# Two changes of issue order in a decoder layer: factor splits of the first matrix pair, and the place of one background job

## The chip, the cores and the metric

The kernel runs on one core of a Trainium2 chip. The metric is device time in microseconds of one execution; three executions of the kernel before gave 1956.08, 1957.77 and 1959.51, so its median is 1957.77 us. The engines are named as in the profile: PE multiplies matrices, DVE and ACT work on vectors, POOL does little here, SP issues the DMA transfers.

## The reference

One layer of a decoder over 512 tokens of width 2048, in fp32:

```python
for l in range(DEPTH):                       # DEPTH = 1
    h = rms_norm(x, norm1_g[l])
    proj = h @ w_in[l]
    qa, ka, va, ra, ga, qb, kb, vb = jnp.split(proj, split_points, axis=-1)
    gate_pre = (ga @ gla_gate_w2[l] + gla_gate_b[l]).astype(jnp.float32)
    log_g = jax.nn.log_sigmoid(gate_pre) / GLA_GATE_TAU
    out_a = gla_mixer(...)                   # gated linear attention, 4 heads
    ...
    out_b = dilated_mixer(...)               # dilated window attention, 8 heads
    mix = jnp.concatenate([out_a, out_b], axis=-1)
    x = x + mix @ w_out[l]
    h2 = rms_norm(x, norm2_g[l])
    x = x + (jax.nn.silu(h2 @ w_gate[l]) * (h2 @ w_up[l])) @ w_down[l]
```

The hidden width of the last line is 5632. Nearly all the work is in the five matrix products.

## The kernel before

**Products.** Each fp32 product is done in a rounded format with a correction: every operand is split in a *high* part, cast by ACT, and a *low* part, the remainder, computed by DVE. For the left factor that is `Operand.split` (L175 the cast, L176 the remainder); for a weight tile the two lines are L311 and L315, or L403 and L407 in the first pair, with results `wh` and `wl`. The matrix products are grouped in pairs of 512-column blocks and carried out by a seven-product scheme in the manner of Strassen: products P1 to P7, whose left factors are the quarters A11, A12, A22 of the operand or their sums and differences S1 to S4, and whose right factors are weight quarters or differences of them (L397 in the first pair, L227 later). Each product runs over four groups of the inner dimension, numbered 0 to 3. One group of one product is an *item*: eight matmuls with `wh` (two terms, the left factor's high and low part) and then four with `wl`.

**First pair.** `first_pair` handles the first pair by hand. Its products come in the order P1, P2, P5, P6, P3, P7, P4, so 28 items numbered k from 0: k = 8 is P5 group 0, k = 9 is P5 group 1 (it needs S1 of group 1, called S1.1), and P4, which needs A22, is k = 24 to 27. In each item the weight splits for the item after are issued, then the eight high matmuls, then one row of the table `FIRST` (the row of item k is number k + 2, counted from 0), then the four low ones. A row is a list of tokens: `S1.1` splits a factor, `+S1.1` computes the sum that is split (L730), `A22.1` splits that quarter, `t.` tokens transpose input, `sq.` tokens are squares for the norm (L643 on ACT), `gate.0` and `gate.1` are `ranks`, 32 small matmuls each (L775), of which gate.1 multiplies the factors A22 and S1. Every engine works strictly in the order in which its instructions were written.

**Later pairs.** They run through `stream`, which calls the pair's `step` between the high and low matmuls of an item. A step advances generators on the list `background`; the first on the list that does not answer "wait" is served first. An item whose factor is not yet split forces the background on until it is.

**The end of the out-projection.** The last item of the second out-projection pair is P4 group 3; after it comes the gate/up pair that I call ffn0 (P1 groups 0 to 3, then P5, P6, P3 and so on). While the out-projection is being closed, rows of x1 are finished on DVE (L1414, L1411), squared (L1447) and scaled (L1422) on ACT, transposed on PE (L1135), copied by ACT with the norm's gain (L1146) and stored to a DRAM tile `xn_d` (L1150). They come back as operand tiles: `early_jobs` loads a tile `top` in two halves of the tokens (L1196), splits its first half as A11, subtracts (L1234) and splits the difference as S3. `late_jobs` loads other tiles (L1250, L1196 into `r`) and makes S1, S2 and S4 and A22. For groups 2 and 3 both jobs are appended to `background` when `which == 1 and half == 1` in `final_out`. Groups 0 and 1 were listed before, as `operand_jobs`.

**Transfers.** SP issues all of these loads and stores in one line, the weight loads (L184) among them, and before each it waits until the transfer eight before it has landed.

Of the kernel before, what the change touches and what calls it, by code (L numbers as in the profile page):

```python
# [43 lines left out]
    "t.l4 +S3.0 t.u1",  # L44
    "t.u3 t.u4 A12.0 A11.3 A12.1 A11.2",
    "t.l5 S2.0 t.l3 +S1.2 +S4.0",
    "S1.2 t.u7 A22.1 t.u5 A12.2",
    "A12.3 t.l6 +S2.2",
    "+S3.2 sq.1.2 S4.0",
    "t.l7 t.l2 +S1.3",  # L50
    "S1.3 sq.1.3",
    "+S1.1 sq.0.1 sq.0.3 A22.2 sq.1.0 +S2.3 sq.0.2",
    "S1.1 sq.2.3 sq.1.1 sq.0.0 g2",
    "normA.0 sq.3.1 sq.3.2 sq.2.1 +S2.1 sq.3.0",
    "A22.3 +S3.1 normB.0 S2.1 normC.0 +S3.3 gprep",
    "S2.2 sq.2.0 seeda sq.3.3 sq.2.2",
    "S2.3 normA.1 +S4.3 normB.1 +S4.1 gate.0",
    "normC.1 +S4.2",
    "closea S3.2 seedb gate.1",
    "S4.1 S3.1",  # L60
    "",
    "S4.2 S4.3",
    "S3.0",
    "seedc",
    "",
    "S3.3",
    "closec",
    "",
    "",
    "",  # L70
# [38 lines left out]
def block_kernel(ctx: ExitStack, tc: tile.TileContext, ins, out):  # L109
# [19 lines left out]
    def nm(s):  # L129
        uid[0] += 1  # L130
        return f"{s}_{uid[0]}"
# [7 lines left out]
    def work(tag, shape=(P, 512), bufs=1):  # L139
        return mp.tile(list(shape), F32, name=nm(tag), tag=tag, bufs=bufs)  # L140

    def const(shape, name):
        return cp.tile(list(shape), F32, name=name, tag=name)
# [345 lines left out]
    background = []  # L489
# [4 lines left out]
    def later(units, fn, hold=False):  # L494

        deferred.append([units, fn, hold])
# [78 lines left out]
    g2 = const([P, 16], "g2")  # L575
# [119 lines left out]
    for g in range(4):  # L695
        for b in (2 * g, 2 * g + 1):
            if g < 3:
                t = apool.tile([P, 2, 512], F32, name=nm("xT"), tag="A")
# [495 lines left out]
    def part_load(t, src, half):  # L1194
        assert (id(src), half) in done
        load(t, src[:, :, half * 256 : (half + 1) * 256])  # L1196
        return t

    def staged(items, ahead=1, cost=1.0, groups=3):

        queue = []
        for keys, fetch, use in items:
            while len(queue) > ahead or not all(key in done for key in keys):
                if queue and ripe(queue[0][2], groups):
                    t, u, when = queue.pop(0)
                    u(t)
                    yield cost
                else:
                    yield WAIT
            queue.append((fetch(), use, now[0]))  # L1210
        while queue:
            if ripe(queue[0][2], groups):
                t, u, when = queue.pop(0)
                u(t)
                yield cost
            else:
                yield WAIT

    def early_jobs(op, groups, tops, flip):

        h0, h1 = (1, 0) if flip else (0, 1)
        items = []
        for g in groups:
            hold = []

            def fetch(g=g, hold=hold):
                t = apool.tile([P, 2, 2, 256], F32, name=nm("top"), tag="A")
                part_load(t[:, 0], tops[g], h0)
                part_load(t[:, 1], tops[g], h1)
                hold.append(t)  # L1230
                return t

            def differ(t, g=g):
                nc.vector.tensor_tensor(t[:, 1], t[:, 0], t[:, 1], op=ALU.subtract)  # L1234
                op.split("S3", g, t[:, 1])

            items.append((
                [(id(tops[g]), 0), (id(tops[g]), 1)], fetch, lambda t, g=g: op.split("A11", g, t[:, 0])
            ))
            items.append(([], lambda hold=hold: hold[0], differ))  # L1240
        return staged(items, 2, 0.5)
# [150 lines left out]
    def residual_loads(rows, c0, src, room="qk"):  # L1392

        res = []
        for m in range(2):
            if room == "L":
                r = work("L", bufs=2)
            elif room == "C":
                r = cpool.tile([P, 512], F32, name=nm("rows"), tag="C")
            else:  # L1400
                r = work(room[m])
            load(r, src(rows[m], c0))
            res.append(r)
        return res

    def residual(tiles, acc_, rest):
        res = []
        for m in range(2):
            r = rest[m]
            if tiles is None:  # L1410
                nc.vector.tensor_tensor(halves(r), unfolded(acc_[m]), halves(r), op=ALU.add)  # L1411
                res.append(r)
            else:
                nc.vector.tensor_tensor(tiles[m], tiles[m], r, op=ALU.add)  # L1414
                res.append(tiles[m])
        return res
# [9 lines left out]
    def final_out(second):  # L1426
        rest_of = {}

        def ahead(half, which):
            tok = 1 - half  # L1430
            rest_of[half, which] = residual_loads(
                [2 * tok, 2 * tok + 1], 512 * (2 * second + which),
                lambda t, c: x[t * P : (t + 1) * P, c : c + 512],
                "C" if (half, which) == (1, 0) else "qk",
            )

        def final(half, which, tiles, acc_):
            tok = 1 - half
            rows = [2 * tok, 2 * tok + 1]
            ch = 2 * second + which  # L1440
            last = tiles is None
            tiles = residual(tiles, acc_, rest_of.pop((half, which)))
            for m in range(2):
                t = rows[m]
                store(x1_d[t][:, 512 * ch : 512 * ch + 512], tiles[m])
                jk = work("st", (P, DV), bufs=2).bitcast(mybir.dt.bfloat16)
                nc.scalar.activation(  # L1447
                    jk, tiles[m], AF.Square, accum_out=ss2[:, t, ch : ch + 1]
                )
            if second:  # L1450
                def scaled():
                    turn = scaled_store(tiles, rows, tok, xn_d[2 * ch : 2 * ch + 2], 4 * ch)
                    later(2, turn)

                if last:
                    later(4, scaled)
                else:
                    scaled()
                if which == 1 and half == 1:
                    background.append(early_jobs(opn, (2, 3), tops, False))  # L1460
                    background.append(late_jobs(opn, ((2, 3),), tops, bots, False))
                if which == 0 and half == 1:
                    output_scales()
            elif which == 0 and half == 1:
                nc.vector.tensor_tensor(part2, ss2[:, :, 0], ss2[:, :, 1], op=ALU.add)
                first_scale()
                background.append(first_columns())
                background.append(operand_jobs(opn, (0, 1), tops, bots))

        final.ahead = ahead  # L1470
        return final
# [51 lines left out]
    opn = Operand(4)  # L1523
    tops = [xn_d[2], xn_d[3], xn_d[6], xn_d[7]]
# [200 lines left out]
```

## Time and profile before

| what | value |
|---|---|
| median of three executions | 1957.77 us |
| the profiled execution | 1956.06 us |
| its span | 1953.9 us, so 2.2 us lie outside it |
| mean granted clock of PE | 0.999 |
| PE busy | 1922.4 us (98%) |
| DVE busy | 1651.5 us (85%) |
| ACT busy | 1095.6 us (56%) |

Start times are in microseconds from the span's start. In a row of the timeline the first two columns are start and duration of a group, then engine, line, operation, and "out<-in" with the tile names; `x8` counts instructions; `[2.19 <-DVE AS L176]` says that the engine stood idle 2.19 us before the group and what ended that. In a table of windows the columns after the length are the busy times of PE, PE's weight load, DVE, ACT and POOL with instruction counts, then PE's granted clock, the busy share of the DMA engines and GB/s.

### The profile page before, as it was taken

The page shows a single profiled execution, that of the slowest core. Times are in us where ns is not written, and L with a number is a line of the kernel's source. Part 1 is how long each engine was busy: PE and PEld are TensorE (multiplying, and loading weights), DVE is VectorE, ACT ScalarE, POOL GpSimd, SP SyncE. Part 2 cuts the span into 40 slices and gives each one's busy share as a digit, 9 for nine tenths or more (in the row PEclk, how much of TensorE's full clock was granted, in tenths as well). Part 3 has the DMA queues.
Part 4 walks back from the last instruction along what each step waited for, and adds up shares of the span by engine and source line. Part 5 has one row for each costly group of instructions (what it writes and reads, how often), then busy time and mean ns, then how long its engine had stood idle before and what let it go on. Part 6 is the DMA issues. An engine that isn't in the chain of part 4 may idle for free.

```text
span 1953.9 us, 25802 instructions
## 1 busy us (share of the span) xinstructions
PE 1922.4 (98%) x9226; PEld 1670.1 (85%) x9226; DVE 1651.5 (85%) x1855; ACT 1095.6 (56%) x1602; POOL 59.1 (3%) x79
## 2 busy tenths in 40 slices
PE   8999999999999999999999999999999999999999
PEld 6888888888888878888888888888888888888888
DVE  8997787867899889878878878878879989989987
ACT  8564564666775776544545545445446646546443
POOL 0000240010000000000000000000000000000000
PEclk9999999999999999999999999999999999999999
DMA  8458355475676695564564553553555865955762
GB/s 280 135 163 276 104 182 157 130 211 181 194 242 195 207 310 168 165 183 126 176 173 127 175 167 124 176 165 129 173 161 163 300 199 185 317 172 180 258 211 69
DMA packets 237801, 362.02 MB, mean 185 GB/s; under 512 B 18294, under 2 KB 96575, under 8 KB 237672
## 3 DMA queue, kind: packets, MB, share of 16 engines
q1 hardware_dynamic: 237320, 360.16, 58.0%
q8 instruction: 72, 1.18, 0.3%
q14 instruction: 57, 0.47, 0.1%
q10 hardware_dynamic: 352, 0.21, 0.0%
HBM read 298.16 MB, written 64.51 MB: 186 GB/s over the span
## 4 chain that ended last, share of the span: by engine, by line
PE 87%; DVE 7%; DMA 2%; issue 2%; ACT 1%; SPq 0%; POOL 0%; DVEq 0%; ACTq 0%
PE acc L355 78%; PE acc L423 3%; DVE wl L315 2%; DVE wa L227 1%; PE bank L1135 1%; PE bank L990 1%; PE bank L1022 1%; DVE AS L176 1%; DMA x<-in_x 1%; ACT wh L311 0%; PE bank L775 0%; PE bank L1015 0%; DMA top<-xn_d 0%; PE bank L925 0%; PE bank L908 0%
## 5 line engine op out<-in xcount | busy, mean ns | idle before, releaser
L355 PE MATMUL acc<-wh,AS 128*128 128x512 f32 x3008 | 711.4, 379 | 0.0
L355 PEld LDWEIGHTS acc<-wh,AS 128*128 128x128 f32 x3008 | 569.2, 189 | 80.2 <-ACT wh L311 0.5
L311 ACT CAST wh<-wa 128x1024 fp32r<-128x1024 f32 x376 | 394.1, 1049 | 401.6 <-PE acc L355 372.1
L355 PE MATMUL acc<-wh,AA 128*128 128x512 f32 x2256 | 534.4, 380 | 2.2 <-ACT wh L311 1.9
L315 DVE TENSOR_TENSOR wl<-wa,wh 128x1024 fp32r<-128x1024 f32 x376 | 459.2, 1225 | 73.0 <-ACT wh L311 41.2
L355 PEld LDWEIGHTS acc<-wh,AA 128*128 128x128 f32 x2256 | 426.8, 189 | 63.9 <-ACT wh L311 3.3
L355 PE MATMUL acc<-wl,AS 128*128 128x512 f32 x1504 | 395.7, 386 | 6.9 <-DVE wl L315 6.7
L355 PEld LDWEIGHTS acc<-wl,AS 128*128 128x128 f32 x1504 | 279.5, 189 | 57.7 <-DVE wl L315 16.9
L355 PE MATMUL acc<-wl,AA 128*128 128x512 f32 x1128 | 295.9, 385 | 1.2 <-DVE wl L315 1.0
L355 PEld LDWEIGHTS acc<-wl,AA 128*128 128x128 f32 x1128 | 210.0, 189 | 32.2 <-DVE wl L315 3.7
L311 ACT CAST wh<-wb 128x1024 fp32r<-128x1024 f32 x94 | 98.6, 1049 | 125.7 <-PE acc L355 120.3
L311 ACT CAST wh<-wc 128x1024 fp32r<-128x1024 f32 x94 | 98.4, 1047 | 112.9 <-PE acc L355 105.6
L311 ACT CAST wh<-wd 128x1024 fp32r<-128x1024 f32 x94 | 98.6, 1049 | 106.6 <-PE acc L355 104.6
L227 DVE TENSOR_TENSOR wa<-wc,wa 128x1024 f32<-128x1024 f32 x94 | 115.1, 1227 | 49.8 <-DMA wc<-in_w_gate 27.7
L315 DVE TENSOR_TENSOR wl<-wd,wh 128x1024 fp32r<-128x1024 f32 x94 | 114.8, 1224 | 39.0 <-ACT wh L311 33.3
L315 DVE TENSOR_TENSOR wl<-wc,wh 128x1024 fp32r<-128x1024 f32 x94 | 115.2, 1225 | 34.0 <-ACT wh L311 33.8
L315 DVE TENSOR_TENSOR wl<-wb,wh 128x1024 fp32r<-128x1024 f32 x94 | 114.2, 1223 | 5.5 <-ACT wh L311 5.5
L227 DVE TENSOR_TENSOR wb<-wd,wb 128x1024 f32<-128x1024 f32 x94 | 115.3, 1227 | 0.7 <-DMA wd<-in_w_in 0.3
L227 DVE TENSOR_TENSOR wa<-wb,wa 128x1024 f32<-128x1024 f32 x94 | 114.0, 1223 | 0.8
L227 DVE TENSOR_TENSOR wa<-wd,wa 128x1024 f32<-128x1024 f32 x94 | 113.6, 1226 | 0.0
L272 DVE SCALAR_TENSOR_TENSOR seed<-acc,rs,seed 128x512 f32<-128x512 f32 x96 | 70.8, 749 | 23.3 <-PE acc L355 23.3
L256 ACT ACTIVATE seed<-acc,rs 128x512 f32<-128x512 f32 x96 | 60.6, 682 | 0.8 <-PE acc L355 0.8
(316 smaller groups left out, 1369.6 us busy)
## 6 DMA issues: line engine op xcount, KB each, us to landing
wa<-in_w_gate SPq DMA_DIRECT2D x44, 512.0 KB, 4.5
wb<-in_w_up SPq DMA_DIRECT2D x44, 512.0 KB, 4.5
wd<-in_w_up SPq DMA_DIRECT2D x44, 512.0 KB, 4.4
wc<-in_w_gate SPq DMA_DIRECT2D x44, 512.0 KB, 3.6
wc<-in_w_in SPq DMA_DIRECT2D x32, 512.0 KB, 3.8
wa<-in_w_in SPq DMA_DIRECT2D x24, 512.0 KB, 5.3
wb<-in_w_in SPq DMA_DIRECT2D x24, 512.0 KB, 5.8
wd<-in_w_in SPq DMA_DIRECT2D x24, 512.0 KB, 6.5
```

The lines of the kernel that those rows point to most:

```text
L176: nc.vector.tensor_tensor(a[:, :, 1, :], src, a[:, :, 0, :].bitcast(F32), op=ALU.subtract)
L227: nc.vector.tensor_tensor(src, self.quarter(one, g), src, op=ALU.subtract)
L256: nc.scalar.activation(halves(t), unfolded(src[m]), AF.Copy, scale=self.scale(half, m))
L272: nc.vector.scalar_tensor_tensor(halves(seed[m]), unfolded(src[m]), self.scale(half, m), halves(seed[m]), op0=ALU.mult, op1=ALU.add,)
L311: nc.scalar.copy(high[k], sources[k])
L315: nc.vector.tensor_tensor(low[k], sources.pop(k), high[k].bitcast(F32), op=ALU.subtract)
L355: nc.tensor.matmul(p.dst[prod][m], a[:, jj, hl, m * P : (m + 1) * P], folded(w[:, jj, :]), start=fresh and g == 0 and len(terms) == 2 and ...
L423: recent["pe"] = nc.tensor.matmul(dst[prod][m], a[:, jj, hl, m * P : (m + 1) * P], folded(w[:, jj, :]), start=fresh and g == 0 and len(ter ...
L990: nc.tensor.matmul(lp[:, :n], qh[:, b * P : (b + 1) * P], kh[:, :n], start=True, stop=True)
L1022: nc.tensor.matmul(op, vh[:, k, :], lgs[b][:, k * P : (k + 1) * P], start=(k == 0), stop=(k == b))
L1135: nc.tensor.transpose(bk[:, jj, m * P : (m + 1) * P], tiles[m][:, f : f + P], ident)
```

## The change

In `FIRST`, A22.1, A22.2 and A22.3 are split ten or more rows later, S1.1 is split right behind its sum and so ahead of four squares, and gate.1 moves from row 16 to row 25, that is from item k = 14 to k = 23. In `final_out`, `early_jobs` of groups 2 and 3 is put at the head of the background list, not at its end.

```diff
@@ -44,27 +44,27 @@
     "t.l5 S2.0 t.l3 +S1.2 +S4.0",
-    "S1.2 t.u7 A22.1 t.u5 A12.2",
+    "S1.2 t.u7 t.u5 A12.2",
     "A12.3 t.l6 +S2.2",
     "+S3.2 sq.1.2 S4.0",
     "t.l7 t.l2 +S1.3",
     "S1.3 sq.1.3",
-    "+S1.1 sq.0.1 sq.0.3 A22.2 sq.1.0 +S2.3 sq.0.2",
-    "S1.1 sq.2.3 sq.1.1 sq.0.0 g2",
+    "+S1.1 S1.1 sq.0.1 sq.0.3 sq.1.0 +S2.3 sq.0.2",
+    "sq.2.3 sq.1.1 sq.0.0 g2",
     "normA.0 sq.3.1 sq.3.2 sq.2.1 +S2.1 sq.3.0",
-    "A22.3 +S3.1 normB.0 S2.1 normC.0 +S3.3 gprep",
+    "+S3.1 normB.0 S2.1 normC.0 +S3.3 gprep",
     "S2.2 sq.2.0 seeda sq.3.3 sq.2.2",
     "S2.3 normA.1 +S4.3 normB.1 +S4.1 gate.0",
     "normC.1 +S4.2",
-    "closea S3.2 seedb gate.1",
+    "closea S3.2 seedb",
     "S4.1 S3.1",
-    "",
+    "A22.1",
     "S4.2 S4.3",
-    "S3.0",
-    "seedc",
+    "S3.0 A22.2",
+    "seedc A22.3",
     "",
     "S3.3",
-    "closec",
+    "closec gate.1",
...
@@ -1457,7 +1457,7 @@
                 if which == 1 and half == 1:
-                    background.append(early_jobs(opn, (2, 3), tops, False))
+                    background.insert(0, early_jobs(opn, (2, 3), tops, False))
                     background.append(late_jobs(opn, ((2, 3),), tops, bots, False))
```

**ACT around S1.1.** Tile names end in numbers. Here are ACT's instructions of before, from the `wh` of k = 8 (of `wa_118`) to that of k = 10 (of `wa_129`); `wa_121` is the weight tile of k = 9, `AA_97_601` is A22.2 and `AS_102_626` is S1.1:

```order
L403 CAST wh_583<-wa_118 128x1024
L643 ACTIVATE L_597,ss_102<-x_112 128x512
L643 ACTIVATE L_599,ss_102<-x_114 128x512
L175 CAST AA_97_601<-xT_166 128x2x256
L643 ACTIVATE L_604,ss_102<-x_110 128x512
L643 ACTIVATE L_607,ss_102<-x_124 128x512
L403 CAST wh_613<-wa_121 128x1024
L175 CAST AS_102_626<-xT_163 128x2x256
L643 ACTIVATE L_629,ss_102<-x_135 128x512
L643 ACTIVATE L_631,ss_102<-x_112 128x512
L643 ACTIVATE L_633,ss_102<-x_110 128x512
L403 CAST wh_642<-wa_129 128x1024
```

The same stretch now, where `AS_94_594` is S1.1:

```order
L403 CAST wh_580<-wa_118 128x1024
L175 CAST AS_94_594<-xT_163 128x2x256
L643 ACTIVATE L_597,ss_102<-x_112 128x512
L643 ACTIVATE L_599,ss_102<-x_114 128x512
L643 ACTIVATE L_601,ss_102<-x_110 128x512
L643 ACTIVATE L_604,ss_102<-x_124 128x512
L403 CAST wh_610<-wa_121 128x1024
L643 ACTIVATE L_623,ss_102<-x_135 128x512
L643 ACTIVATE L_625,ss_102<-x_112 128x512
L643 ACTIVATE L_627,ss_102<-x_110 128x512
L403 CAST wh_636<-wa_129 128x1024
```

The cast of S1.1 has moved ahead of four squares and of the `wh` of k = 9. The squares still stand between the `wh` of k = 8 and that of k = 9, four in number as before, but all of them are now behind the cast of S1.1. Its low part moves on DVE too, to the place right behind its sum, where A22.2's low part stood.

**SP at the second place.** These are the transfers around the closing of the out-projection, before. `xn_d_207` and `xn_d_208` are the DRAM tiles of groups 2 and 3; their second token halves are the two stores from `oT` and `PT`. `top_6772` and `top_6775` are the tiles of `early_jobs`:

```order
L184 DMA wb_6908<-in_w_up 128x2x512
L184 DMA wb_6941<-in_w_up 128x2x512
L1150 DMA xn_d_207<-oT_6638 256x1x256
L1150 DMA xn_d_208<-PT_6647 256x1x256
L184 DMA wd_6962<-in_w_up 128x2x512
L184 DMA wd_6999<-in_w_up 128x2x512
L1250 DMA T_6894<-xn_d_208 128x2x256
L1445 DMA x_d_199<-seed_6085 128x512
L1445 DMA x_d_200<-seed_6106 128x512
L1250 DMA v_6786<-xn_d_207 128x2x256
L184 DMA wd_7024<-in_w_up 128x2x512
L1196 DMA top_6772<-xn_d_207 128x2x256 x2
```

The same stretch now (`top_6651` and `top_6654`):

```order
L184 DMA wb_6902<-in_w_up 128x2x512
L1196 DMA top_6651<-xn_d_207 128x2x256
L184 DMA wb_6931<-in_w_up 128x2x512
L1150 DMA xn_d_207<-oT_6638 256x1x256
L1150 DMA xn_d_208<-PT_6647 256x1x256
L184 DMA wd_6958<-in_w_up 128x2x512
L1196 DMA top_6651<-xn_d_207 128x2x256
L1196 DMA top_6654<-xn_d_208 128x2x256 x2
L1445 DMA x_d_199<-seed_6085 128x512
L1445 DMA x_d_200<-seed_6106 128x512
L1250 DMA T_6950<-xn_d_208 128x2x256
L184 DMA wd_6995<-in_w_up 128x2x512
```

The first load of `top` now goes out between two weight loads, ahead of the stores. The other three come right behind the stores and one weight load, ahead of the stores of x1 (`x_d`), of the load of `T`, and of the second and third load of `wd`.

**DVE and ACT at the second place.** On DVE, from the low part of P4 group 3's weights (`wl_6723`, of `wa_6006`) to that of the second item of ffn0 (`wl_6798`), before, and one row further; `wl_6744` belongs to the first item:

```order
L315 TENSOR_TENSOR wl_6723<-wa_6006,wh_6719 128x1024
L176 TENSOR_TENSOR AS_1314_6712<-qT_6483,AS_1314_6712 128x2x256
L176 TENSOR_TENSOR AA_1318_6733<-kT_6549,AA_1318_6733 128x2x256
L315 TENSOR_TENSOR wl_6744<-wa_6721,wh_6740 128x1024
L1411 TENSOR_TENSOR rows_6674<-acc_5965,rows_6674 128x512
L1411 TENSOR_TENSOR rows_6676<-acc_5966,rows_6676 128x512
L315 TENSOR_TENSOR wl_6798<-wa_6742,wh_6794 128x1024
L1234 TENSOR_TENSOR top_6772<-top_6772 128x512
```

Now, from the same low part of P4 group 3 (`wl_6729`) on; `wl_6754` belongs to the first item of ffn0:

```order
L315 TENSOR_TENSOR wl_6729<-wa_6006,wh_6725 128x1024
L176 TENSOR_TENSOR AS_1304_6659<-v_6448,AS_1304_6659 128x2x256
L1234 TENSOR_TENSOR top_6651<-top_6651 128x512
L1350 TENSOR_TENSOR v_6448<-kT_6549,v_6448 128x512
L1234 TENSOR_TENSOR top_6654<-top_6654 128x512
L315 TENSOR_TENSOR wl_6754<-wa_6727,wh_6750 128x1024
L176 TENSOR_TENSOR AS_1309_6685<-v_6448,AS_1309_6685 128x2x256
L176 TENSOR_TENSOR AS_1316_6718<-qT_6483,AS_1316_6718 128x2x256
L176 TENSOR_TENSOR AA_1320_6739<-top_6651,AA_1320_6739 128x2x256
L176 TENSOR_TENSOR AS_1321_6743<-top_6651,AS_1321_6743 128x2x256
L1411 TENSOR_TENSOR rows_6680<-acc_5965,rows_6680 128x512
L176 TENSOR_TENSOR AA_1329_6782<-top_6654,AA_1329_6782 128x2x256
```

Both differences of `top` (L1234), which need the loads, now stand ahead of the first item's `wl`. On ACT, from the `wh` of the first item of ffn0 (`wh_6740`) to that of the third (`wh_6831`), before:

```order
L311 CAST wh_6740<-wa_6721 128x1024
L1146 ACTIVATE oT_6759<-bank_6754,g_91 128x256 x2
L1146 ACTIVATE PT_6768<-bank_6763,g_91 128x256 x2
L311 CAST wh_6794<-wa_6742 128x1024
L1447 ACTIVATE st_6811,ss_209<-rows_6674 128x512
L1447 ACTIVATE st_6814,ss_209<-rows_6676 128x512
L175 CAST AA_1340_6828<-top_6772 128x2x256
L311 CAST wh_6831<-wa_6796 128x1024
```

Now, from the `wh` of the first item (`wh_6750`) to that of the second (`wh_6794`):

```order
L311 CAST wh_6750<-wa_6727 128x1024
L175 CAST AS_1309_6685<-v_6448 128x2x256
L175 CAST AS_1316_6718<-qT_6483 128x2x256
L175 CAST AA_1320_6739<-top_6651 128x2x256
L175 CAST AS_1321_6743<-top_6651 128x2x256
L1146 ACTIVATE oT_6769<-bank_6764,g_91 128x256 x2
L1146 ACTIVATE PT_6778<-bank_6773,g_91 128x256 x2
L175 CAST AA_1329_6782<-top_6654 128x2x256
L175 CAST AA_1330_6785<-kT_6549 128x2x256
L311 CAST wh_6794<-wa_6752 128x1024
```

Before, the first cast of `top` stood ahead of the third item's `wh`. Now three casts of `top`, and the two casts of S4.1 and S3.1 (`AS` from `v` and `qT`), stand between the first item's `wh` and the second's.

## The prediction, made before the changed kernel was run

> **What bounds the kernel now.** I read the page first, then the waits of PE, then the timeline where PE waits. The page:
>
> ```profile
> span 1953.9 us, 25802 instructions
> ...
> PE 1922.4 (98%) x9226; PEld 1670.1 (85%) x9226; DVE 1651.5 (85%) x1855; ACT 1095.6 (56%) x1602; POOL 59.1 (3%) x79
> ```
>
> PE is busy 98% of the span, and the change alters no PE work, so only what PE waits can move the time. The waits of PE in the first 150 us (first row) and from 700 to 765 us (in all, times, longest):
>
> ```profile
> PE acc L423 <- DVE AS L176: 2.2, 1, 2.2
> ...
> PE acc L355 <- ACT wh L311: 1.9, 1, 1.9
> ```
>
> The first is PE waiting for S1.1's low part, the second for a `wh` behind a cast of `top`: both parts of the change touch a wait. The profiled execution took 1956.06 us, 1.71 below the median 1957.77; I sum against the former and add the difference.
>
> **First place: S1.1 ahead of the squares.** PE (with the window of its clock), DVE and ACT there:
>
> ```profile
> 40.41 0.46 PE L423 MATMUL acc<-wh,AS 128*128 128x512 f32 x1
> 43.06 3.36 PE L423 MATMUL acc<-wh,AS 128*128 128x512 f32 x7 [2.19 <-DVE AS L176]
> ...
> 43.00:44.00 1.00, 0.94 (x2) 0.84 (x3) 1.00 (x3) 1.00 (x4) 0.00 (x0) 0.50 1.04 404
> ...
> 32.05 0.69 DVE L730 TENSOR_TENSOR xT<-xT,xT 128x512 f32<-128x512 f32 x1 [0.37 <-ACT xT L680]
> ...
> 38.25 0.68 DVE L730 TENSOR_TENSOR xT<-xT,xT 128x512 f32<-128x512 f32 x1
> ...
> 42.33 0.68 DVE L176 TENSOR_TENSOR AS<-xT,AS 128x512 fp32r<-128x512 f32 x1
> ...
> 47.53 1.23 DVE L407 TENSOR_TENSOR wl<-wa,wh 128x1024 fp32r<-128x1024 f32 x1 [0.17 <-ACT wh L403]
> ...
> 39.72 0.61 ACT L175 CAST AS<-xT 128x512 fp32r<-128x512 f32 x1
> 40.24 0.63 ACT L643 ACTIVATE L<-x 128x512 bf16<-128x512 f32 x1
> ...
> 42.09 1.03 ACT L403 CAST wh<-wa 128x1024 fp32r<-128x1024 f32 x1
> ...
> 46.46 1.04 ACT L403 CAST wh<-wa 128x1024 fp32r<-128x1024 f32 x1 [0.88 <-PE acc L423]
> ```
>
> Item k = 9 issued one matmul at 40.41 and waited until 43.06. The sum +S1.1 runs on DVE at 38.25 and ends at 38.93. It will not run earlier: the only removed work before it, A22.1's low part, lies before 32.05, where DVE waited 0.37 us for ACT anyway. ACT now meets S1.1's cast first and must wait for 38.93. Then follow, by the steps between the ACT rows, the cast (40.24 - 39.72 = 0.52), four squares at (42.09 - 40.24) / 3 = 0.62, and k = 9's `wh`, 1.03 long: 38.95 + 0.52 + 2.47 + 1.03 = 43.0. So S1.1's low part is early (about 40.1), but now `wh` is what is late, at nearly the same time. PE starts k = 9 at 43.0 with 12 matmuls to do, where before 11 were left at 43.06: +0.2 us (one matmul, 0.22, less 0.06).
>
> What is late next: ACT. Behind that `wh` stand three squares and k = 10's `wh`, four squares and k = 11's `wh`: 42.95 + 1.85 + 0.95 + 2.47 + 1.03 = 49.3, the short 0.95 being the start-to-start step of a `wh`. Before, it came at 46.46 and ended at 47.5; so DVE's `wl` of k = 11 moves from 47.53 to 49.35, 1.8 us later.
>
> **First place: gate.1 and A22 moved.** PE, and DVE with its idle times from k = 16 on:
>
> ```profile
> 63.02 2.06 PE L775 MATMUL bank<-AA,gs 128*128 128x256 f32 x16
> ...
> 66.80 1.03 PE L423 MATMUL acc<-wl,AS 128*128 128x512 f32 x4
> ...
> 75.43 1.89 PE L423 MATMUL acc<-wh,AS 128*128 128x512 f32 x8
> ...
> 67.94 1.23 DVE L407 TENSOR_TENSOR wl<-wd,wh 128x1024 fp32r<-128x1024 f32 x1 [2.16 <-PE acc L423]
> ...
> 70.67 1.23 DVE L407 TENSOR_TENSOR wl<-wd,wh 128x1024 fp32r<-128x1024 f32 x1 [0.31 <-ACT wh L403]
> ...
> 73.26 1.23 DVE L407 TENSOR_TENSOR wl<-wd,wh 128x1024 fp32r<-128x1024 f32 x1 [1.36 <-ACT wh L403]
> 74.41 1.29 DVE L176 TENSOR_TENSOR AS<-xT,AS 128x512 fp32r<-128x512 f32 x2
> ```
>
> gate.1 held PE for 66.80 - 63.02 = 3.78 us in k = 14. While it ran, DVE gained a lead. Without it k = 18 (at 75.43, it needs S4.2, the first of the two at 74.41) would start at 75.43 - 3.78 + 0.2 = 71.85. DVE from 47.53 to 74.41 took 26.88 us, of which the three idle times above are 3.83; A22.3's low part leaves this stretch and A22.1's, equally long, enters. From 49.35 without idling that gives 49.35 + 23.05 = 72.4, and S4.2's low part is done at 73.0. The second matmul of k = 18 wants it at 71.85 + 0.22 = 72.07, so PE waits 0.9. Behind k = 18, A22.2 and A22.3 add 2 x 0.6 on DVE, which is just covered (by the same steps `wl` of k = 20 ends at about 79.4, and is wanted at 79.7) until gate.1 in k = 23 gives DVE its 3.78 us back. The three A22 casts cost nothing: ACT idled beside them, as the 1.36 and 0.31 that DVE waited for a `wh` come from ACT waiting for PE. SP and POOL are not involved.
>
> The whole first part: 0.2 + 0.9, about **+1.0 us**. Bounds: +0.2 if DVE saves 0.9 somewhere, and +1.8 if all of the 1.8 that `wl` of k = 11 is late reaches PE. A gain below +0.2 I leave to a rival.
>
> **Second place: `top` first in line.** ACT, DVE, PE, then DVE's load as a window:
>
> ```profile
> 722.90 0.83 ACT L1146 ACTIVATE oT<-bank,g 128x256 f32<-128x256 f32 x2
> ...
> 728.79 0.62 ACT L175 CAST AA<-top 128x512 fp32r<-128x512 f32 x1 [2.16 <-DMA top<-xn_d]
> ...
> 729.54 0.69 DVE L1234 TENSOR_TENSOR top<-top 128x512 f32<-128x512 f32 x1 [2.90 <-DMA top<-xn_d]
> ...
> 725.75 1.89 PE L355 MATMUL acc<-wh,AA 128*128 128x512 f32 x8
> ...
> 730.40 2.34 PE L355 MATMUL acc<-wh,AA 128*128 128x512 f32 x8 [1.90 <-ACT wh L311]
> ...
> 761.52 0.81 PE L355 MATMUL acc<-wh,AS 128*128 128x512 f32 x3
> ...
> 729.50:757.50 28.00, 24.59 (x110) 19.75 (x111) 27.96 (x33) 19.11 (x27) 6.08 (x5) 1.00 0.52 168
> ```
>
> After the load at 728.77 DVE is busy 27.96 of 28.00 us, and PE 24.59. DVE sets the pace, so the gain is what DVE idles less before 757.5, not what PE waits at 730. The transfers (issue on SP; and issue to landing of the second store, of `top`, and of loads of the same size later; the window shows the transfer rate before):
>
> ```profile
> 713.30 0.52 SPq L1150 DMA_DIRECT2D xn_d<-PT  x1
> ...
> 718.89 0.57 SPq L1250 DMA_DIRECT2D T<-xn_d  x1
> ...
> 721.99 1.39 SPq L1196 DMA_DIRECT2D top<-xn_d  x2
> ...
> DMA to landing us min/median/max: 5.5/5.5/5.5
> ...
> DMA to landing us min/median/max: 6.8/6.8/6.8
> ...
> DMA to landing us min/median/max: 3.0/3.4/3.9
> ...
> 705.00:718.00 13.00, 12.72 (x63) 10.90 (x62) 12.97 (x19) 10.85 (x19) 0.00 (x0) 1.00 1.04 373
> ```
>
> The store landed at 713.30 + 5.5 = 718.8, and `T` went out behind it. Now a quarter of a megabyte more (the first load of `top`) lies ahead: 0.26 MB at 373 GB/s, 0.7 us, so about 719.5. The last of the other three loads goes out 0.6 later, at some 720.1. Its landing is the unknown: 3.0 to 3.9 us where the queue is light, 6.8 where `top` stood behind two x1 stores, `T`, `v` and two weight loads. Now one weight load lies ahead of it. I take 3.1, nearest the light end, so 723.2.
>
> From there, with 0.61 for a DVE step of 512 columns (1.29 for the two at 74.41, less 0.68 for the last) and 1.15 for one of 1024 (74.41 - 73.26): the second L1234 ends at 723.8 and `wl` of P1 group 0 at 725.0, so that PE gets this low part about half a microsecond late. ACT follows L1350 with the casts of S4.1, S3.1 and two of `top` from 723.4 (2.1 us), four L1146 (0.83 for two, 1.6), two casts (1.0) and `wh` (1.03): P1 group 1 starts at about 729.1, against 725.75 before, after an idle 3.1 us. That is the price: PE is 3.4 us later here. It is given back, since PE no longer waits at group 2, and DVE's pace decides: its idling is 2.6 us now (its other work ends at 720.6 by the steps above, the load lands at 723.2), where it was 3.9 between 720 and 730, the 2.90 above and these two:
>
> ```profile
> 721.57 0.69 DVE L176 TENSOR_TENSOR AS<-qT,AS 128x512 fp32r<-128x512 f32 x1 [0.80 <-ACT AS L175]
> ...
> 723.03 1.23 DVE L315 TENSOR_TENSOR wl<-wa,wh 128x1024 fp32r<-128x1024 f32 x1 [0.17 <-ACT wh L311]
> ```
>
> 3.9 less 2.6 is **-1.3 us**: P3 group 0 at 760.2 for 761.52. The ends: -1.8 if the last load goes out without the 0.7 of delay, at 719.5, and takes 3.2 (landing at 722.7), and +2.4 if it takes 6.8 us again (720.1 + 6.8 = 726.9, 3.7 later than assumed).
>
> **The clock after a gap of 3.1 us.** After 2.19 us of idling the clock was 0.50 at 43 us, and seven matmuls took 3.36 us. Elsewhere it was not touched by more:
>
> ```profile
> 484.39 0.30 PE L1015 MATMUL bank<-mats,L 128*128 128x128 f32 x1 [3.02 <-DVE L L1006]
> ...
> 485.00:486.00 1.00, 1.00 (x7) 0.87 (x6) 0.94 (x4) 0.63 (x2) 0.00 (x0) 1.00 0.00 0
> ```
>
> The length of a gap alone does not decide. If the clock halves at 729, seven matmuls take the 3.36 us of 43.06, where at full clock eight take 1.89 and so seven 1.65: 1.7 more. PE had 28.00 - 24.59 = 3.4 us idle in DVE's window, of which P1 group 2 starting at 731.7 (729.1 and an item of 2.6) for 730.40 takes 1.3; the 1.7 fits into the rest, and I take 0, with 1.7 as the other end. The Trainium skill, "TensorE: Matmul & The Clock Gate", Part 1, says that the clock falls after an idle window of about 3.4 us and that this window runs freely. By that rule a gap of 3.1 us cannot halve the clock, and the end of 1.7 falls away. The trace agrees for the 3.02 us, and contradicts it for the 2.19 us.
>
> **The sum.** +1.0 - 1.3 = -0.3 us: 1955.8 for the profiled execution, 1957.5 for the median.
>
> **The rivals.**
> *The change doesn't act at the second place* (the loads land, but `wl` and `wh` held behind them cost what DVE saves): +1.0 alone, 1958.8. For it: the 3.4 us by which P1 group 1 starts later. Against: DVE's 27.96 of 28.00. 15 in 100.
> *Slower: `top` lands late.* Now `wl` of P1 group 0 and `wh` of group 1 stand behind the loads, so each microsecond after 723.2 delays DVE and PE alike. At 6.8 us from issue it lands at 726.9: +2.4 there, +1.0 at the first place, and a gap of 6.8 us before P1 group 1 with up to 1.7 of half clock: 1961.2 to 1962.9, the middle 1962.0. For it: the store and `top` of this very stretch took 5.5 and 6.8. Against: what queued ahead of `top` is now behind it. It decides, with half of the 1.7, from a landing at 726.5 on. 24 in 100, of which 20 beyond +3.9.
> *Faster: the wait at 43 goes.* If `wh` of k = 9 is ready by 40.41, the 2.19 us and the 1.7 of half clock go: -3.9, and -1.3 at the second place: -5.2, 1952.6. For it: S1.1's low part, named as the releaser, comes 2.3 us sooner. Against: 2.47 us of squares before `wh` on ACT. 10 in 100, and 3 more for a second place that gives more than I see.
>
> **Chances and range.** My forecast has 48 in 100. 0.2%, 3.9 us, is about what a measurement of this kernel can tell from no change. Faster than that: the last rival, 13. Slower: the late landing beyond 3.9, 20. The rest, 67, lies within. The range begins at 1953.8: the best ends of both places, +0.2 - 1.8, make 1956.2, less the 1.7 by which executions fell below the median 1954.5, and 0.7 for a part of the faster case. It ends at 1962.0 with half of the late landing.
>
> **What would show it.** First place: PE's wait before k = 9 some 2.4 us, released by ACT's `wh` (L403), not by DVE's S1.1; a wait of up to 1 us before k = 18; nothing at 63. Second place: `top`'s last load landing near 723; PE idle some 3 us before P1 group 1, released by ACT `wh`; no wait at P1 group 2; P3 group 0 near 760 once the first place's +1.0 is taken off. I am wrong if k = 9 starts before 42, or if the load lands after 725.

## The result, and the profile after

Seven executions of the changed kernel have a median of 1965.82 us (1963.47 to 1967.89), seven of the kernel before, beside them, 1958.31. The ratio is 1.0039, with a 95% interval of 1.0028 to 1.0051: slower by some 7.6 us, where 1957.5 and at most 1962.0 had been forecast. Of the executions of the variants below one, of the kernel with the second part alone, took 4131.07 us and is left out of its ratio. The profiled execution took 1966.57 us. Its page, the part with the busy times:

```profile
span 1964.8 us, 25807 instructions
...
PE 1928.1 (98%) x9226; PEld 1671.2 (85%) x9226; DVE 1652.1 (84%) x1855; ACT 1095.5 (56%) x1602; POOL 63.2 (3%) x79
```

DVE and ACT do what they did before, and PE is busy 5.7 us more, most of it half clock; the rest of the 10.9 us of longer span is waiting. POOL, which does next to nothing, has 4.1 us more. The waits of PE, first from 700 to 780 us, then in the first 150 us:

```profile
PE acc L355 <- DVE wl L315: 5.2, 3, 3.5
PE acc L355 <- ACT AS L175: 4.4, 1, 4.4
...
PE acc L423 <- ACT wh L403: 3.3, 3, 2.5
PE acc L423 <- ACT seed L437: 1.2, 1, 1.2
```

To see where the time came from I take, for each matmul of PE, its start after minus its start before. This offset is +0.93 at 88 us, behind the first place; it gains 1.7 at 485 to 487, where the code is the same but the clock is not (last section), and goes up to 3.7 by 692 and back. It is 2.77 at 725.82, where the second place begins (P1 group 0), and 11.0 at its end (P3 group 0 starts at 772.52, before at 761.52). So the second place costs 8.2 of the 10.9. What the second place costs in a run is taken between these two matmuls from here on.

**First place.** PE from k = 9 on; the third row is k = 11, the last k = 12:

```profile
42.85 1.99 PE L423 MATMUL acc<-wh,AS 128*128 128x512 f32 x8 [2.51 <-ACT wh L403]
...
45.64 1.99 PE L423 MATMUL acc<-wh,AS 128*128 128x512 f32 x8
...
49.03 2.00 PE L423 MATMUL acc<-wh,AS 128*128 128x512 f32 x8 [0.54 <-ACT wh L403]
...
53.05 2.14 PE L423 MATMUL acc<-wh,AS 128*128 128x512 f32 x8 [1.16 <-ACT seed L437]
```

k = 9 waits for its `wh`, as forecast, and eight matmuls then take 1.99 us, so the clock was not halved this time. PE then waits for ACT twice more, at k = 11 and k = 12. There is no wait at k = 18.

**Second place.** PE around the two long waits, and two windows with its clock (the column after POOL's):

```profile
725.82 1.89 PE L355 MATMUL acc<-wh,AA 128*128 128x512 f32 x8
731.26 1.91 PE L355 MATMUL acc<-wl,AA 128*128 128x512 f32 x4 [3.54 <-DVE wl L315]
733.05 2.88 PE L355 MATMUL acc<-wh,AA 128*128 128x512 f32 x8
737.20 1.13 PE L355 MATMUL acc<-wl,AA 128*128 128x512 f32 x4 [1.27 <-DVE wl L315]
...
747.66 1.03 PE L355 MATMUL acc<-wl,AS 128*128 128x512 f32 x4
753.05 4.08 PE L355 MATMUL acc<-wh,AS 128*128 128x512 f32 x8 [4.37 <-ACT AS L175]
...
732.00:733.00 1.00, 1.00 (x3) 0.36 (x2) 1.00 (x3) 1.00 (x2) 0.00 (x0) 0.50 1.01 389
...
754.00:755.00 1.00, 1.00 (x3) 0.82 (x4) 1.00 (x2) 0.00 (x0) 0.00 (x0) 0.50 0.00 0
```

The first wait is the low part of P1 group 0. Four low matmuls then take 1.91 us for 1.03: half clock. By 747.66, P5 group 1, the offset is +5.06, so this wait has cost 2.3 net. The second is P5 group 2, which waits for the factor S1.2, again with half clock behind it (eight matmuls in 4.08 for 1.89). It takes the offset to 11.0: 5.9 more. In the runs below without the second wait PE makes up 0.5 to 1.5 us between these two places, so the share of the first wait is rather less than 2.3 and that of the second more than 5.9. The two have different causes.

*The first wait: `top` lands late.* The transfers, with their issue on SP, and DVE:

```profile
716.28 0.53 SPq L1150 DMA_DIRECT2D xn_d<-oT  x1
717.06 0.52 SPq L1150 DMA_DIRECT2D xn_d<-PT  x1
...
722.82 1.92 SPq L1196 DMA_DIRECT2D top<-xn_d  x3
...
726.06 0.69 DVE L1234 TENSOR_TENSOR top<-top 128x512 f32<-128x512 f32 x1 [2.79 <-DMA top<-xn_d]
...
729.38 0.69 DVE L1234 TENSOR_TENSOR top<-top 128x512 f32<-128x512 f32 x1 [2.02 <-DMA top<-xn_d]
729.99 1.22 DVE L315 TENSOR_TENSOR wl<-wa,wh 128x1024 fp32r<-128x1024 f32 x1
```

The store issued at 716.28 lands just before 722.82, 6.5 us later. The three loads of `top` go out from there to 724.14. The first lands 3.2 us after its issue. The last lands at 729.3, when DVE takes it up: 5.2 us after its issue, behind 0.5 MB of the other two. DVE's `wl` of P1 group 0 stands behind that load.

*The second wait: a chain that the prediction didn't look at.* ACT's seed at the closing of P1 (L256) multiplies by the row scale of the second norm. That scale comes from the squares of the finished rows (L1447), two tiny sums on DVE (L1516, L1517), and five instructions on POOL (L159, L160, L1519 to L1521: an inverse square root over 4 columns). POOL, ACT, then DVE from the second tiny sum on, in the changed kernel:

```profile
739.12 8.52 POOL L159 TENSOR_SCALAR rs<-tmp 128x4 f32<-128x4 f32 x1 [279.21 <-DVE tmp L1517]
747.72 0.20 POOL L1519 TENSOR_SCALAR part<-part 128x4 f32<-128x4 f32 x1
...
750.05 0.20 POOL L1521 TENSOR_TENSOR rs<-rs,part 128x4 f32<-128x4 f32 x1
...
750.29 1.27 ACT L256 ACTIVATE seed<-acc,rs 128x512 f32<-128x512 f32 x2 [6.50 <-POOL rs L1521]
751.44 1.04 ACT L311 CAST wh<-wa 128x1024 fp32r<-128x1024 f32 x1
752.38 0.62 ACT L175 CAST AS<-r 128x512 fp32r<-128x512 f32 x1
...
738.88 0.15 DVE L1517 TENSOR_TENSOR tmp<-tmp,part 128x4 f32<-128x4 f32 x1
738.95 1.22 DVE L227 TENSOR_TENSOR wa<-wb,wa 128x1024 f32<-128x1024 f32 x1
...
746.37 1.21 DVE L227 TENSOR_TENSOR wa<-wb,wa 128x1024 f32<-128x1024 f32 x1
753.03 0.69 DVE L176 TENSOR_TENSOR AS<-r,AS 128x512 fp32r<-128x512 f32 x1 [5.45 <-ACT AS L175]
```

A POOL instruction on 4 columns lasts 8.52 us and ends at 747.64, as DVE falls idle at 747.58 after eight instructions without a pause; its fellow L1519, just as small, takes 0.20 right behind it, with DVE idle. ACT waits 6.5 us for POOL, the cast of S1.2 stands behind that, DVE waits for the cast, and PE for all of them. Before, the same POOL instruction was over in 1.10 us, between two long instructions of DVE (the last two lines):

```profile
731.07 1.10 POOL L159 TENSOR_SCALAR rs<-tmp 128x4 f32<-128x4 f32 x1 [272.05 <-DVE tmp L1517]
...
736.54 0.85 POOL L1521 TENSOR_TENSOR rs<-rs,part 128x4 f32<-128x4 f32 x1
...
730.90 1.22 DVE L227 TENSOR_TENSOR wa<-wb,wa 128x1024 f32<-128x1024 f32 x1
732.04 1.22 DVE L315 TENSOR_TENSOR wl<-wa,wh 128x1024 fp32r<-128x1024 f32 x1
```

With the change the tiny sums come 5.3 us later on DVE (738.20 for 730.15, less the offset), behind the factors of `top`, and POOL's first instruction then met a DVE that didn't let it in.

### The profile page after: what moved, and what is told of

It is laid out like the page before. It is cut to its first block, busy times and chain, and to the rows that moved or that the text cites. A ratio compares the mean times of both kernels' runs of the same rounds, so it can differ in the third digit from the quotient of the medians.

```text
span 1964.8 us, 25807 instructions
## 1 busy us (share of the span) xinstructions
PE 1928.1 (98%) x9226; PEld 1671.2 (85%) x9226; DVE 1652.1 (84%) x1855; ACT 1095.5 (56%) x1602; POOL 63.2 (3%) x79
## 4 chain that ended last, share of the span: by engine, by line
PE 81%; DVE 6%; DMA 3%; issue 1%; ACT 1%; POOL 1%; SPq 0%; DVEq 0%; ACTq 0%; POOLq 0%
PE acc L355 76%; DVE wl L315 2%; DVE wa L227 1%; PE bank L1135 1%; PE bank L990 1%; PE bank L1022 1%; DMA x_d<-seed 1%; DMA xn_d<-oT 1%; DVE AS L176 0%; POOL rs L159 0%; PE bank L1015 0%; DMA xn_d<-PT 0%; DMA T<-p_d 0%; DMA wd<-in_w_up 0%; PE bank L908 0%
## 5 line engine op out<-in xcount | busy, mean ns | idle before, releaser
L256 ACT ACTIVATE seed<-acc,rs 128x512 f32<-128x512 f32 x96 | 60.8, 684 | 7.3 <-POOL rs L1521 6.5
```

The costliest lines, as they stand in the source:

```text
L256: nc.scalar.activation(halves(t), unfolded(src[m]), AF.Copy, scale=self.scale(half, m))
```

## The experiments

**Each part alone.** The first run has only the change of the table, the second only this:

```diff
-                    background.append(early_jobs(opn, (2, 3), tops, False))
+                    background.insert(0, early_jobs(opn, (2, 3), tops, False))
```

> Only the table of the first pair is changed; the background job is appended at the end as before. My theory (the loss lies at the second place, where the load of top lands late and the row scale that POOL computes is late): PE reaches the second pair about 0.6 to 1.4 us later than before, no wait over 2 us between 700 and 770 us besides that of before, 0.0% to 0.1% slower in all. Rival (the loss lies in the first pair, or in both places alike): 0.2% slower or more.

Measured: 1958.20 us against 1956.72, 1.0004 [0.9994, 1.0013]. The offset behind the first place is +1.19, and the second place costs nothing (the offset falls by 0.95 there).

> Only the background job is put at the head of the list; the first pair is as before. My theory: nearly the whole loss, 6 to 9 us (0.3% to 0.45%), with a wait of about 3.5 us for the low part of P1 group 0 and one of about 4.4 us for a cast that stands behind the closing of P1 on ACT, which waits for POOL. Rival (the two parts only hurt together, or the loss lies in the first pair): within 0.15% of the time before.

Measured: 1962.54 us against 1956.72, 1.0026 [1.0017, 1.0035]. Most of the loss is the second place's. The profiled execution was the lowest of them (1957.25), and its trace does not show the second wait: DVE happened to pause for 0.47 us in it, and POOL's L159 ended then, after 3.37 us. So POOL's wait seems to last until DVE pauses.

**The scale without its chain.** If the second wait is the scale's, it must go when the seed needs no POOL. In the first version the scale is that of the first norm, long ready (the second norm's is left out):

> The changed kernel, but the row scale of the gate/up and later products is read from the first norm's scales, which have been ready for long, so nobody waits for what POOL computes at the second place; POOL still computes it. This leaves out the second norm's scale from the result. My theory: the wait of 4.4 us before P5 group 2 and the half clock after it go, and the kernel is 4 to 6 us faster than the changed one, so 0.05% to 0.25% slower than the time before; POOL's first instruction there is still long. Rival (ACT or DVE would be late there anyway, through the casts put in front): the wait stays within 1 us of 4.4.

Measured: 1958.45 us against 1956.72, 1.0002 [0.9992, 1.0012]. PE's waits from 720 to 780 us:

```profile
PE acc L355 <- DVE wl L315: 3.6, 1, 3.6
PE acc L355 <- ACT wh L311: 0.8, 1, 0.8
```

The wait for S1.2 is gone, that for P1 group 0 is there as in the changed kernel, and the second place costs 2.6 us (offset 2.31 to 4.88). What is left is the first wait. In this execution too DVE paused (0.46 us), and POOL's chain ended at 744.93, just ahead of the seed at 744.98; so it is the time of the ten executions, more than this trace, that shows the seed's wait for POOL to be the cause. In the second version the true scale is computed by DVE and ACT:

```diff
-        rsqrt_mean(rs2, tmp2, D)
-        nc.gpsimd.tensor_scalar(part2, part2, 2.0 / D, EPS, op0=ALU.mult, op1=ALU.add)
-        nc.gpsimd.tensor_tensor(part2, part2, phalf, op=ALU.pow)
-        nc.gpsimd.tensor_tensor(rs2, rs2, part2, op=ALU.mult)
+        nc.vector.tensor_scalar(tmp2, tmp2, 1.0 / D, EPS, op0=ALU.mult, op1=ALU.add)
+        nc.vector.tensor_scalar(part2, part2, 2.0 / D, EPS, op0=ALU.mult, op1=ALU.add)
...
+            nc.scalar.activation(tmp2, tmp2, AF.Ln)
+            nc.scalar.activation(part2, part2, AF.Ln)
+            nc.vector.tensor_tensor(tmp2, part2, tmp2, op=ALU.subtract)
...
+        soon(lambda: nc.scalar.activation(rs2, tmp2, AF.Exp, scale=0.5), 2)
```

> The changed kernel with the second norm's row scale computed by DVE and ACT (sum, logarithms, exponential), in place of POOL's five instructions. Theory (POOL is kept waiting by DVE's unbroken run of instructions with two inputs, and ACT then waits for POOL): ACT's wait before the closing of P1 falls from 6.5 us to under 1, PE's wait of 4.4 us before P5 group 2 goes, and the time falls by 5 to 7 us against the changed kernel, to within 0.1% of the time before. Rival (the scale is late because its sums of squares are late, whoever computes it): a wait of 3 us or more stays at that place.

Measured: 1957.86 us against 1957.06, 1.0004 [0.9994, 1.0014]. L256 runs at 738.91 without waiting, and the second place costs 0.4 us. The change without POOL's wait takes about the time that had been forecast, with no difference from before that can be measured. It gets there by another way: PE still waits 2.4 us for P1 group 0.

**`top` without its late landing.** Here `early_jobs` loads the rows of groups 0 and 1, stored long before, so that the loads of `top` don't wait for the stores (A11 and S3 of groups 2 and 3 are then those of other rows):

```diff
-                part_load(t[:, 0], tops[g], h0)
-                part_load(t[:, 1], tops[g], h1)
+                src = tops[g] if flip else tops[g % 2]
+                part_load(t[:, 0], src, h0)
+                part_load(t[:, 1], src, h1)
```

> The changed kernel, but the job of groups 2 and 3 loads the rows of groups 0 and 1, which were stored earlier, so its four loads do not wait for the two stores just issued; the same number of loads of the same size. This leaves groups 2 and 3 of A11 and S3 wrong in the result. My theory: PE's wait of 3.5 us at the low part of P1 group 0 goes, DVE does not idle over 1 us between 719 and 730, the sums of squares end some 5 us sooner, and the time falls by 3 us or more against the changed kernel; if POOL then finds DVE as busy, its first instruction is still several us long, but the wait behind it is shorter. Rival (the casts and differences put ahead are the cost, not the landing of the loads): within 1 us of the changed kernel.

Measured: 1961.24 us against 1956.72, 1.0018 [1.0009, 1.0027], some 4 us less than the changed kernel. The place in the line is then worth much: nobody waits for `top`, and the offset falls from 4.12 to 0.18 by 742.78. But POOL waits longer still, and the offset rises to 5.9:

```profile
733.42 9.12 POOL L159 TENSOR_SCALAR rs<-tmp 128x4 f32<-128x4 f32 x1 [273.17 <-DVE tmp L1518]
...
PE acc L355 <- ACT AS L175: 4.2, 1, 4.2
```

With both causes removed (these loads, and the scale by DVE and ACT):

> The loads of groups 2 and 3 take the rows of groups 0 and 1, which do not wait for the stores (this leaves A11 and S3 of two groups wrong in the result), and the row scale is computed by DVE and ACT. Theory (two costs, the landing of the loads and POOL, ate what the place in line gave): DVE does not idle between 719 and 730, and the second place gives 2 to 4 us, so 0.05% to 0.15% faster than before with the first place's 1 us. Rival (the place in line gives nothing): within 0.05% of before, or slower.

Measured: 1952.75 us against 1955.23, 0.9988 [0.9978, 0.9997]. DVE does not idle between 719 and 730, and the offset goes from 2.66 to -2.16 at the second place: -4.8 us. So the first place in line does help, if the loads come early and POOL is not waited for; in the changed kernel the real rows are stored too late for that (from 716.28 on).

**What lets POOL in.** Three versions put small instructions of no use between DVE's long ones. First a tiny sum and four reductions, each of one input with 512 columns:

```diff
+        nc.vector.tensor_tensor(spare1, tmp2, tmp2, op=ALU.add)
+        for _ in range(4):
+            nc.vector.tensor_reduce(
+                spare1[:, :1], mats.rearrange("p a b -> p (a b)"), axis=mybir.AxisListType.X, op=ALU.add
+            )
```

> The changed kernel with four reductions of 512 columns added on DVE, one between each two of the next weight instructions behind the last sum of squares; they have one input, where the instructions around them have two. Some 2.5 us of work more on the engine that sets the pace. Theory (an instruction of DVE with two inputs from SBUF shuts POOL out, one with a single input lets it in): POOL's first instruction ends with the first reduction, within 3 us of its start for 8.5, PE's wait before P5 group 2 falls below 2.5 us, and the time falls by 2 to 5 us although work was added. Rival (any unbroken run on DVE keeps POOL waiting, or POOL is slow by itself): POOL's first instruction takes 8 us or more and the time rises by 1 to 3 us.

Measured: 1962.36 us against 1957.06, 1.0024 [1.0015, 1.0033]. That is some 3 us less than the changed kernel, though some 2.5 us were added to DVE, which sets the pace; the two intervals still overlap a little. POOL gets through, and the wait for S1.2 is gone:

```profile
738.61 1.11 POOL L159 TENSOR_SCALAR rs<-tmp 128x4 f32<-128x4 f32 x1 [277.67 <-DVE tmp L1517]
739.80 1.12 POOL L1519 TENSOR_SCALAR part<-part 128x4 f32<-128x4 f32 x1
...
744.41 1.27 ACT L256 ACTIVATE seed<-acc,rs 128x512 f32<-128x512 f32 x2
```

Then four instructions with two inputs, of 384 columns, in the place of the reductions:

```diff
+        nc.vector.tensor_tensor(old[:, :4], tmp2, tmp2, op=ALU.add)
+        for _ in range(4):
+            nc.vector.tensor_tensor(old, old, old, op=ALU.max)
```

> As the run with the four reductions, but in their places stand four additions of work with two inputs from SBUF (a maximum of 384 columns with itself, in place, on constants that are no longer needed). Theory (only an instruction with a single input, or one of a few elements, lets POOL in): POOL passes one instruction at the small sum of four columns, as there, but its second or third waits until DVE idles, 4 us or more; PE's wait before P5 group 2 is back at 3 us or more, and the time is 1 us or more above that of the run with the reductions. Rival (POOL gets in at the end of any instruction once the order of widths is mixed, as in the order of before): every instruction of POOL is done within 2 us, and the time is within 1 us of the run with the reductions.

Measured: 1964.37 us against 1955.23, 1.0048 [1.0033, 1.0063]. POOL gets in once, beside the tiny sum at 736.25, and then not for 9.27 us, until DVE runs dry at 745.69. ACT waits 7.82 us. The widths are mixed here as in the kernel before, so a mix of widths alone does not let POOL in:

```profile
735.28 1.11 POOL L159 TENSOR_SCALAR rs<-tmp 128x4 f32<-128x4 f32 x1 [274.62 <-DVE tmp L1517]
736.47 9.27 POOL L1519 TENSOR_SCALAR part<-part 128x4 f32<-128x4 f32 x1
...
748.12 1.26 ACT L256 ACTIVATE seed<-acc,rs 128x512 f32<-128x512 f32 x2 [7.82 <-POOL rs L1521]
```

Last, five of the tiny sums alone, which cost DVE 0.08 us each:

```diff
+        for _ in range(5):
+            nc.vector.tensor_tensor(spare1, tmp2, tmp2, op=ALU.add)
```

> As the run with the four reductions, but with sums of four columns in their places, 0.1 us each. Theory (a gap lets POOL in): POOL's instructions each end within 2 us of their start, its chain takes under 7 us for 11, ACT's wait behind it falls below 2 us, and the time falls by 4 to 6 us against the changed kernel. Rival (only long instructions with a single input give POOL time enough): POOL's chain takes 9 us or more and the time stays within 1.5 us of the changed kernel.

Measured: 1956.65 us against 1955.23, 1.0007 [0.9998, 1.0017]. Five sums of 4 columns take some 6 us off the changed kernel (1.0039 without them). POOL's first two instructions end beside the first two of the sums:

```profile
736.60 1.11 POOL L159 TENSOR_SCALAR rs<-tmp 128x4 f32<-128x4 f32 x1 [276.38 <-DVE tmp L1517]
737.79 1.13 POOL L1519 TENSOR_SCALAR part<-part 128x4 f32<-128x4 f32 x1
...
737.57 0.15 DVE L1524 TENSOR_TENSOR spare<-tmp 128x4 f32<-128x4 f32 x1
...
738.78 0.15 DVE L1524 TENSOR_TENSOR spare<-tmp 128x4 f32<-128x4 f32 x1
```

**The four squares ahead of S1.1's cast.** The rival in which the wait at 43 us goes had four squares on ACT against it. Here these four stand ahead of S1.1's cast, where ACT does them while it waits for the sum, and other squares move behind the first seeds; the rest is the kernel before, with the other moves of the table kept:

```diff
-    "+S1.1 sq.0.1 sq.0.3 A22.2 sq.1.0 +S2.3 sq.0.2",
-    "S1.1 sq.2.3 sq.1.1 sq.0.0 g2",
-    "normA.0 sq.3.1 sq.3.2 sq.2.1 +S2.1 sq.3.0",
...
+    "+S1.1 sq.0.1 sq.0.3 sq.1.0 +S2.3 sq.0.2 S1.1",
+    "sq.1.1 sq.0.0 g2",
+    "normA.0 +S2.1",
...
+    "S2.2 seeda sq.2.3 sq.3.1 sq.3.2",
```

> The kernel before with another table for the first pair: A22 and gate.1 late as in the change, but S1.1 is split behind four squares, which ACT can do while it waits for the sum, and the other squares move behind the first seeds. The background job stays at the end of its list. Theory (what kept the stall at 43 us alive was ACT's four squares and the wh behind S1.1's cast): PE starts k = 9 near 40.6 without a wait over 0.3 us, there is no half clock after it, and the second pair starts 1.5 to 4 us earlier than before; 0.1% to 0.2% faster. Rival (the splits of the first pair are bound by DVE, so the wait comes back elsewhere before the second pair): the second pair starts within 0.7 us of before.

Measured: 1956.11 us against 1957.06, 1.0000 [0.9991, 1.0009]. The wait at 43 does go (offset -3.5 at 45.8), but PE then waits further on, and -0.5 is left by 87:

```profile
PE acc L423 <- ACT seed L437: 1.3, 1, 1.3
...
PE acc L423 <- ACT wh L403: 0.9, 1, 0.9
...
PE acc L423 <- DVE AS L176: 0.6, 1, 0.6
```

This table, the first place in line and the scale by DVE and ACT together:

> The table of the run just before, the background job at the head of its list as in the change, and the second norm's row scale on DVE and ACT. Theory: the gain of the first pair stays (1.5 to 4 us) and the second place costs nothing any more or gains 1 us: 0.1% to 0.25% faster than before. Rival (the late landing of top still costs its 2 us or more at the second place): no faster than before by more than 0.1%.

Measured: 1956.36 us against 1957.06, 0.9995 [0.9986, 1.0003]: not to be told from the kernel before. The low part of P1 group 0 still waits 3.5 us for `top`.

## Why the prediction was wrong

**The first place: right in size, wrong in place.** +1.0 was forecast; the offset shows +1.2 with the table alone and +0.9 in the changed kernel. The wait for `wh` before k = 9 was forecast at some 2.4 and is 2.5. The next delay was sought on DVE at k = 18, when the one on ACT that the text itself had worked out (`wh` of k = 11 some 1.8 later) reaches PE at once, at k = 11, and the seeds of k = 12 behind it.

**The second place, "DVE's pace decides: -1.3": wrong, +8.2.** The rule itself held; the idling put into it, 2.6 us, did not. From 717 to 775 us DVE idles 10.8 us in the changed kernel (2.79, 2.02, 5.45, 0.37 and 0.21), 7.0 more than the 3.9 of before, and the place costs 8.2. With the first place alone it idles 2.9 (0.95 less, for -0.95), and with early loads and the scale by DVE and ACT not at all (3.9 less, for -4.8). So the rule gives the cost to within 1.3 us. The idling was misjudged twice.

The smaller part is the landing. The step took 3.1 us from the last issue, "nearest the light end", and got 5.2; the store took 6.5 for 5.5, and the issue came later too. Less the 2.77 of offset the last load landed at 726.5, not 723.2, just where the rival of the late landing was said to decide. Its price there, +2.4, was on the high side: DVE did one difference and L1350 between the landings, and its two idle times, 4.8 for 3.9, are 0.9 more. In the five profiled executions with this landing in which PE does not wait for POOL and no long work was added on DVE, the second place costs 0.4 to 2.6 us. The place differs too: PE lost the time before the low part of P1 group 0, not before P1 group 1. The 5.2 lies between the light rows (3.0 to 3.9) and the 6.8 of `top` itself, as the loads now lay behind each other. The 6.8 was also read with one transfer too many: of the two weight loads said to lie ahead of `top`, the first, issued at 714.92, took 6.8 us and so had landed by 721.7, just before `top` went out at 721.99.

The larger part, +5.9 (5.45 of DVE's idling), is in no term of the sum and in none of the rivals. The step asked when DVE and ACT would be ready, and did not follow who else was waiting behind the work that was moved ahead. The norm's scale was: two sums on DVE, then POOL, then ACT's seed, then S1.2. That POOL is not involved was said of the first place; the second place's part does not name it, though the trace of before had marks of what happened:

```profile
202.99 4.05 POOL L862 COPY decay<-L 128x8 f32<-128x8 f32 x1 [11.14 <-ACT L L857]
...
288.96 3.40 POOL L159 TENSOR_SCALAR so<-so 128x2 f32<-128x2 f32 x1 [1.13 <-ACT oT L931]
...
304.29 0.19 POOL L862 COPY decay<-L 128x8 f32<-128x8 f32 x1 [11.14 <-ACT L L857]
```

The same copy took 4.05 us once and 0.19 another time.

**The clock, "I take 0".** Both long waits of the second place halved it, and half clock is part of the 2.3 and of the 5.9; the end of 1.7 was the right one. At 43 us, where 2.19 us had halved it before, 2.51 us did not. The row at 484 us, which the text set against that, shows the rarer case: the clock fell there in ten of thirteen profiled executions (last section).

**The rivals.** The faster one was rightly held unlikely: where the wait at 43 does go, 3.0 of the 3.5 us come back as waits on ACT and DVE within 45 us. The late landing came true, but with the first place and no other cost it would have given some 1957.8 + 1.2 + 2.3 = 1961.3, within the range. Of the sum, 1.2 + 2.3 + 5.9 = 9.4, the medians show 7.6; an execution varies by more than that difference.

**What stays open.** What was shown is that POOL can be kept waiting for as long as DVE runs long instructions of two inputs without a pause, and that an idle DVE, an instruction of one input, or one of 4 columns lets it in. Not shown is why it was let in between such instructions in the kernel before (731.07, at the change of DVE's instruction at 732.04) and in the run with the table alone, and not in the changed order. The ends and starts of DVE's instructions look alike there, the next starting some 0.08 us before the end recorded for the last, in both.

## What to carry to other kernels

Work that is put first in line delays whatever stood there: follow each chain behind it to its end, through the idle engine that does the few small steps of a norm, and ask at what it will meet a busy one. A small POOL instruction beside a busy DVE has no fixed price: look in the trace for the longest of its kind, not the median, and don't have ACT wait for it behind a stretch in which DVE has no pause, or put a few tiny instructions there. And a load that goes out third in a row is priced by a row in which it stood third.

## What the runs showed of the hardware

The same POOL instruction of 4 columns (L1519) took 0.20 us with DVE idle, and 9.27 us beside the two-input maxima. ACT's wait of 6.50 us in the changed kernel ends with POOL's chain. The Trainium skill, "SBUF — State Buffer", Who interferes with whom, says that DVE and GpSimd share a pair of ports under an exclusive lock, that a DVE instruction with two inputs in SBUF contends with a GpSimd instruction that reads there, and that `tensor_reduce` doesn't on this chip. The traces agree as to the kinds (1.12 us to the start of a reduction, 9.27 beside the two-input maxima). But the page has the one wait for the other's whole instruction, and here POOL waited through eight of them, 8.52 us, and once through eleven, 9.27.

The clock after a gap is not fixed by its length, nor by the place. At 484 us PE waits 3.0 us in both kernels, for the same work. Before, the clock stayed at 1.00 behind it; in the changed kernel's execution it fell to 0.50:

```profile
486.00:487.00 1.00, 1.00 (x4) 0.77 (x3) 0.55 (x2) 0.23 (x2) 0.00 (x0) 0.50 0.00 0
```

Of the thirteen profiled executions of this case it stayed at 1.00 in three, that of the kernel before among them, and fell to 0.50 in ten (behind a gap of 2.6 us in one of these), with each of the three tables of the first pair. That is 1.7 us between two profiles that is due to no change. A difference between two profiles has to be read place by place before it is given to an edit.
